# Where the first norm's sums of squares are made: ScalarE on token-major rows instead of GpSimd on transposed ones

## The chip, the cores and the metric

The kernel runs on one core of one Trainium2 chip. Its time is the device time of one execution in microseconds (us); of the kernel before, three runs are shown: 1096.92, 1096.26 and 1096.07 us, with a median of 1096.26 us.

In the rows of the trace the engines are PE (TensorE, matrix products), PEld (its weight loads), DVE (VectorE), ACT (ScalarE), POOL (GpSimd) and SP (SyncE, which issues nearly all DMAs; SPq is its queue). A line such as L109 is a line of the kernel's source.

## The reference, cut to what matters

One encoder layer on 256 tokens of width 2048, all in float32. Its first step is the one that the change touches:

```python
def rms_norm(x, g):
    y = xf * lax.rsqrt(jnp.mean(xf * xf, axis=-1, keepdims=True) + NORM_EPS)
    return (y * g).astype(x.dtype)

h = rms_norm(x, norm1_g)
proj = h @ w_in                     # 2048 x 4640: q, k, v, the gated part's q, k, v, gate, two low ranks
...                                 # windowed attention on one half, gated linear attention on the other
x = x + concat(o_attn, o_gla) @ w_out
x = x + conv_gated_ffn(rms_norm(x, norm2_g), w_up, conv_w, conv_b, w_down)
```

The norm needs, for each token, the sum of the squares of its 2048 values. Since that sum only scales a token's row, the kernel multiplies `x * norm1_g` with `w_in` first and applies 1/rms when the products leave PSUM.

## The kernel before, in words

Every product is made of operands split in two parts (a high part in a reduced format and the rest), three matmuls for one. A weight tile therefore goes through the same steps everywhere, in the helper `weights`: SP loads up to 512 KB into one of four `raw` buffers (L104), ACT writes the high part `hi` (L108, four buffers), DVE writes `lo = raw - hi` (L109, three buffers), and PE takes both. A `raw` buffer is free for the next load when ACT and DVE have read it. A tile's name tells its place: `rikv`, `hikv`, `likv` are raw, high and low of the input projection's first chunk of columns (k and v), `riqa`, `hiqa`, `liqa` those of its second and third chunk (queries).

The input projection runs over ten chunks of columns. Each chunk goes over 16 k-tiles of 128 rows. The first chunk has four units of one k-tile and six of two (called units 0 to 9 here); the second has eight units of two k-tiles (units q0 to q7 here). One k-tile takes six matmuls of 128x512. With the units of the first chunk SP also loads x, transposed (`xts`, L145); ACT scales and rounds it (`hh`, L148) and DVE makes the rest (`hl`, L149).

Hooks put other work between the units: `at(chunk, unit, fn)` calls `fn` before that unit's weights are asked for. There, `token_square(0)` and `(1)` make the squares of all transposed x on GpSimd (L173) and add them by halves (L174 to L176); `token_norm` sums over partitions by eight narrow matmuls with ones (`pn`, L183) and takes the root (`inv_sqrt`, L168 on DVE and L169 on GpSimd); `load_consts` loads the constants `cst_sb` and `prm_sb`; `store(0, ...)` brings the first chunk out of PSUM with the factor `rstd1` (L236). A scheduler orders the instructions on each engine from these calls; the splits of weights and the evacuations have a raised priority.

After the ten chunks come the attention pieces that are woven between them, the output projection (L584 to L586), the up projection with convolution (L632, L633) and the down projection (L667 to L669). PE takes instructions strictly in the order that the schedule gives, and so do the other engines and SP's queue.

Of the kernel before, what the change touches and what calls it, by code (L numbers as in the profile page):

```python
# [8 lines left out]
F32 = mybir.dt.float32  # L9
F32R = mybir.dt.float32r  # L10
BF16 = mybir.dt.bfloat16
U32 = mybir.dt.uint32
AF = mybir.ActivationFunctionType
ALU = mybir.AluOpType
AX = mybir.AxisListType
PSUM = bass.MemoryType.PSUM

A = slice(None)
P = 128
T = 256  # L20
DM = 2048
# [6 lines left out]
EPS = 1e-6  # L28
WCOLS = 1024

# Column chunks of the input projection: (name, [(first column, width), ...], whole width).
IN_CHUNKS = [
    ("kv", [(1024, 512)], 512),
    ("qa0", [(0, 512)], 512),
# [9 lines left out]


def in_units(ci):
    """k-tiles of each weight unit of a chunk of the input projection."""
    return [1] * 4 + [2] * 6 if ci == 0 else [3] * 5 + [1] if ci in (3, 4) else [2] * 8


# Small constants and parameters, by column.
C_COS, C_SIN, C_MASK, C_MF, C_MB = 0, 256, 512, 1024, 1280
C_QG, C_QGS, C_KG, C_KGS = 1536, 1664, 1792, 1920
NCST = 2048
# [5 lines left out]
def tile_hymba_layer(  # L60
# [15 lines left out]
    nc = tc.nc  # L76
    V, S, G, PE = nc.vector, nc.scalar, nc.gpsimd, nc.tensor
# [9 lines left out]
    def arena(shape, dt, name):  # L87
        return ar.tile(shape, dt, name=name, tag="ar")
# [7 lines left out]
    def aux(name):  # L96
        return paux.tile([P, 512], F32, name=name, tag="aux")
# [16 lines left out]
        V.tensor_tensor(lo, src, hi.bitcast(F32), ALU.subtract)  # L114

    def product(d, a, b, start=True, stop=True):
        """d (+)= a^T b, of operands in two parts each."""
        PE.matmul(d, a[0], b[0], start=start, stop=False)
        PE.matmul(d, a[0], b[1], start=False, stop=False)
        PE.matmul(d, a[1], b[0], start=False, stop=stop)  # L120
# [1 line left out]
    def both(tiles, *index):  # L122
        return [x[index] for x in tiles]

# [1 line left out]
    g1 = pers.tile([P, NKT], F32, name="g1")  # L126
    nc.scalar.dma_start(out=g1, in_=n1)
    prm_sb = pers.tile([P, NPRM], F32, name="prm_sb")
# [7 lines left out]
    xts, hh, hl = [], [], []  # L136
# [3 lines left out]
        hl.append(arena([P, 8, T], F32R, f"hl{i}"))  # L140

    def load_x(kt, n):
        """n k-tiles of x, scaled by the first norm's weight and split."""
        i, o = kt // 8, kt % 8
        nc.sync.dma_start(out=xts[i][:, o : o + n], in_=xt[:, kt : kt + n])  # L145
        for j in range(n):
            with tc.high_priority(offset=1500):
                S.activation(hh[i][:, o + j], xts[i][:, o + j], AF.Copy, scale=g1[:, kt + j : kt + j + 1])  # L148
                V.scalar_tensor_tensor(  # L149
                    out=hl[i][:, o + j], in0=xts[i][:, o + j], scalar=g1[:, kt + j : kt + j + 1],  # L150
                    in1=hh[i][:, o + j].bitcast(F32), op0=ALU.mult, op1=ALU.subtract,
                )
# [7 lines left out]
    warm = aux("warm")  # L160
    for i in range(9):
        PE.matmul(warm[:, :P], ones, ones, start=True, stop=True)
    ssq1 = {}
    rstd1 = pers.tile([P, 2], F32, name="rstd1")

    def inv_sqrt(dst, src, mul, add, n):
        t = sm.tile([P, 32], F32, name="isq", tag="isq")
        V.tensor_scalar(t[:, :n], src, mul, add, op0=ALU.mult, op1=ALU.add)  # L168
        G.tensor_tensor(dst, t[:, :n], mhalf[:, :n], op=ALU.pow)  # L169

    def token_square(i):
        sq = arena([P, 8, T], F32, f"sqx{i}")
        G.tensor_tensor(sq, xts[i], xts[i], op=ALU.mult)  # L173
        G.tensor_tensor(sq[:, 0:4], sq[:, 0:4], sq[:, 4:8], op=ALU.add)  # L174
        G.tensor_tensor(sq[:, 0:2], sq[:, 0:2], sq[:, 2:4], op=ALU.add)
        G.tensor_tensor(sq[:, 0], sq[:, 0], sq[:, 1], op=ALU.add)  # L176
        ssq1[i] = sq[:, 0]

    def token_norm():
        pn = aux("pn")  # L180
        for t in range(2):
            for i in range(2):
                PE.matmul(pn[:, 2 * t : 2 * t + 2], ssq1[i][:, t * P : t * P + P], ones[:, 0:2], start=(i == 0), stop=(i == 1))  # L183
        inv_sqrt(rstd1, pn[:, 0:4:2], 1.0 / DM, EPS, 2)

    cst_sb = arena([P, NCST], F32, "cst_sb")
    dec_sb = arena([P, 4, 384], F32R, "dec_sb")
# [11 lines left out]
    def load_wa():  # L199
        nc.sync.dma_start(out=wa_sb, in_=wa)  # L200

# [1 line left out]
    in_first = [0]  # L203

    hooks = {}
# [1 line left out]
    def at(ci, u, fn, *args):  # L207
        hooks.setdefault((ci, u), []).append((fn, args))
# [26 lines left out]
        with tc.high_priority(offset=1500):  # L235
            S.activation(dst, src, func, scale=rstd1[:, t : t + 1])  # L236

# [1 line left out]
    rope_kg = arena([P, 2, 1024], F32, "rope_kg")  # L239
    rope = rope_kg[:, 0].rearrange("p (a b c d) -> p a b c d", a=2, b=2, c=2)  # L240
    kg_sb = rope_kg[:, 1].rearrange("p (t c) -> p t c", t=2)
# [107 lines left out]
        if h % 2 == 1:  # L349
            split(oah[:, h - 1 : h + 1], oal[:, h - 1 : h + 1], po.rearrange("p (k s) -> p k s", k=2))  # L350

# [1 line left out]
    lr_sb = pers.tile([P, 2, 32], F32, name="lr_sb")  # L353
    gkT = arena([P, 2, GH, T], F32, "gkT")
    gh = arena([P, 2, 1024], F32R, "gh")
# [59 lines left out]
                gkT[:, 1, :, t * P : t * P + P], pq.rearrange("p (h s) -> p h s", h=GH), AF.Copy, scale=float(P) ** -0.5  # L415
            )

    # The blocks of e: for a key, -F3, the levels, B3; for a query, -B3, the levels, F3. By direction and tile of
    # tokens: (first column in the bank, role, first column in e, width, sign).
    PARTS = (  # L420
# [19 lines left out]
            V.tensor_tensor(e, e, gkT[:, role, h, t * P : t * P + P].unsqueeze(1).broadcast_to([P, 4, P]), ALU.mult)  # L440

    def mix(h):
        """The decayed products of head h: A^T [s, t] over all pairs of tokens."""
        es = arena([P, 2, 2, 4, P], F32, f"es{h}")
        scaled(h, 0, es)
        yield
        scaled(h, 1, es)
        yield

        def blk(role, t, what):  # L450
            return es[:, role, t, (0, 1 + t, 2 - t, 3)[what]]

        p1 = aux(f"p1{h}")
        p2 = aux(f"p2{h}")
        for s in range(2):
            for t in range(2):
                lv = 2 if s == t else 1
                PE.matmul(p1[:, (2 * s + t) * P : (2 * s + t + 1) * P], blk(0, s, lv), blk(1, t, lv), start=True, stop=True)
        for f in range(2):
            for t in range(2):  # L460
                PE.matmul(p2[:, (2 * f + t) * P : (2 * f + t + 1) * P], blk(0, t, 3 * f), blk(1, t, 3 - 3 * f), start=True, stop=True)
        at = work([P, 4, P], F32, f"at{h}", "sc", 3)
        S.activation(at.rearrange("p a s -> p (a s)"), p1, AF.Copy)
        diag = at[:, 0::3]
        for f, c in enumerate((C_MF, C_MB)):
            V.copy_predicated(
                diag, cst_sb[:, c : c + 256].bitcast(U32).rearrange("p (a s) -> p a s", a=2),
                p2[:, 2 * f * P : (2 * f + 2) * P].rearrange("p (a s) -> p a s", a=2),
            )
        split(atr[0][:, h], atr[1][:, h], at)  # L470
# [26 lines left out]
                PE.transpose(pt[:, e * T + t * P : e * T + t * P + P], o[:, t, e * P : e * P + P], ident)  # L497
        split(ogh[:, 2 * h : 2 * h + 2], ogl[:, 2 * h : 2 * h + 2], pt.rearrange("p (k s) -> p k s", k=2))

# [1 line left out]
    def store(ci, ps):  # L501
        """What a chunk of the projection goes to."""
        for t in range(2):
            if ci >= 8:
                c = ci - 8
                d = sg[:, t, c * 512 : c * 512 + 512]
                evac(d, ps[t], t, AF.Silu)
                dv = d.rearrange("p (h e) -> p h e", h=2)
                V.tensor_tensor(dv, dv, gn.unsqueeze(1).broadcast_to([P, 2, 256]), ALU.mult)
            elif ci == 3:  # L510
                evac(lr_sb[:, t], ps[t][:, 0:32], t)
                evac(kg_sb[:, t, 0:240], ps[t][:, 32:272], t)
            else:
                evac(
                    (kv_sb[:, t], qa_sb[:, 0, t], qa_sb[:, 1, t], None, kg_sb[:, t, 240:512],
                     gq_sb[:, t], vg[:, t, 0:512], vg[:, t, 512:1024])[ci], ps[t], t,
                )
            if ci in (6, 7):
                sl = slice((ci - 6) * 512, (ci - 5) * 512)
                split(vgr[0][:, t, sl], vgr[1][:, t, sl], vg[:, t, sl])  # L520
# [1 line left out]
    running = {}  # L522

    def go(*names):
        """Emit the next stage of each of the named pieces."""
        for name in names:
            if name not in running:
                fn = {"A": attend, "Q": queries, "M": mix, "R": retrieve}.get(name[0])
                running[name] = fn(int(name[1])) if fn else {"k": keys, "g": gates, "gk": gla_keys, "gq": gla_queries}[name]()
            next(running[name], None)  # L530
# [2 lines left out]
        at(0, u, load_x, u, 1)  # L533
    for u in range(4, 10):
        at(0, u, load_x, 2 * u - 4, 2)
    at(0, 7, token_square, 0)
    at(1, 1, token_square, 1)
    at(1, 2, token_norm)
    at(1, 2, load_consts)
    at(1, 4, rope_tables)  # L540
    at(1, 4, go, "k")
    at(2, 0, go, "k")
    at(2, 2, load_decay, 0)
    at(2, 4, load_decay, 1)
# [11 lines left out]
    for (ci, u), names in plan.items():  # L556
        at(ci, u, go, *names.split())
    first_ps = project(0)
    at(1, 3, store, 0, first_ps)
    for ci in range(1, len(IN_CHUNKS)):  # L560
        store(ci, project(ci))

# [1 line left out]
    x1 = [arena([P, 2, 2, 512], F32, f"x1{i}") for i in range(2)]  # L564
    xs = [arena([P, 4, 2, T], F32R, f"xs{i}") for i in range(4)]
    ssq2 = pers.tile([P, 2, 4], F32, name="ssq2")
    first = 0
# [47 lines left out]
    rbc = pers.tile([P, T], F32, name="rbc")  # L615
    V.tensor_copy(rbc, pb[:, :T])

# [1 line left out]
    gts = [arena([P, 2, 4, T], F32R, f"g{i}") for i in range(NFF // 4)]  # L619
    first = 0  # L620
    for f in range(NFF):
# [28 lines left out]
        S.activation(gt[:, 0, f % 4], cs[1], AF.Copy)  # L650
        V.tensor_tensor(gt[:, 1, f % 4], cs[1], gt[:, 0, f % 4].bitcast(F32), ALU.subtract)

# [1 line left out]
    first = 0  # L654
    for c in range(4):
        ps = [acc(f"pd{c}{t}") for t in range(2)]
# [61 lines left out]


def _units(w, sizes):  # L720
    """[K, n] -> units of a few k-tiles, each [128 partitions, k-tiles * n] in one run."""
    n, k, parts = w.shape[1], 0, []
    for per in sizes:
        parts.append(w[k : k + per * P].reshape(per, P, n).transpose(1, 0, 2).reshape(-1))
        k += per * P
    return np.concatenate(parts)
# [54 lines left out]
```

## Time and profile before

| what | value |
|---|---|
| median of three runs | 1096.26 us |
| span of the profiled execution, first to last instruction | 1094.4 us |
| PE busy | 1080.4 us (99%) |
| DVE busy | 783.6 us (72%) |
| ACT busy | 529.7 us (48%) |
| POOL busy | 31.2 us (3%) |
| mean DMA rate | 185 GB/s |

The profile gives the profiled execution's span and no further time of its own; the median of the runs stands 1.9 us above that span. A busy PE says only that a matmul was in flight. The share is a mean over the whole span: of the page's 40 slices of 27 us each, the first has PE at 7 tenths, the second at 8 and all later ones but the last at 9 (90% or more).

### The profile page before, as it was taken

Reading aid. Unit: us, or ns where it says so; the run is one execution under the profiler, and the core shown is the slowest. Engines: PE = TensorE matmul, PEld = TensorE weight load, DVE = VectorE, ACT = ScalarE, POOL = GpSimd, SP = SyncE. Lnnn points to the kernel's source line nnn. Section 1 sums busy time; section 2 is a strip of 40 time slices with the busy share of each in tenths; the row PEclk is TensorE's granted clock in tenths of the full one; section 3 lists DMA queues with packets and bytes.
Section 4 is the critical chain, followed back from the end, with each engine's and each line's share of the span. In section 5 each row is a group of like instructions: output and inputs, shape, how many; then the busy total and the mean of one; then the engine's idle time right before and its main releaser. Section 6 shows DMA issues by size and latency. Waiting matters only on the chain.

```text
span 1094.4 us, 14985 instructions
## 1 busy us (share of the span) xinstructions
PE 1080.4 (99%) x5616; PEld 921.1 (84%) x5616; DVE 783.6 (72%) x1173; ACT 529.7 (48%) x780; POOL 31.2 (3%) x24
## 2 busy tenths in 40 slices
PE   7899999999999999999999999999999999999998
PEld 6789888888888888888888888888888888888886
DVE  7788777756555888888888888888888544444443
ACT  6345566764445544444444444444444433333331
POOL 4311000010000000000000000000000000000000
PEclk9999999999999999999999999999999999999999
DMA  8565544436556655655565565555565656666662
GB/s 302 173 201 165 165 154 148 139 117 187 201 194 219 200 184 184 191 186 184 189 186 184 189 187 182 190 190 179 189 191 181 195 195 210 196 214 196 210 193 79
DMA packets 58040, 202.96 MB, mean 185 GB/s; under 512 B 6576, under 2 KB 7600, under 8 KB 57840
## 3 DMA queue, kind: packets, MB, share of 16 engines
q1 hardware_dynamic: 57680, 201.87, 58.2%
q8 instruction: 44, 0.72, 0.3%
q14 instruction: 28, 0.23, 0.1%
q10 hardware_dynamic: 288, 0.14, 0.0%
HBM read 199.89 MB, written 2.10 MB: 185 GB/s over the span
## 4 chain that ended last, share of the span: by engine, by line
PE 97%; DVE 1%; DMA 1%; ACT 0%; issue 0%; SPq 0%; DVEq 0%; ACTq 0%
PE pu L632 30%; PE pu L633 15%; PE pd L667 7%; PE pd L669 7%; PE pd L668 7%; PE po L586 3%; PE po L584 3%; PE po L585 3%; PE pvg L228 1%; PE pvg L229 1%; PE pqa L229 1%; PE pgt L230 1%; PE pgt L228 1%; PE pvg L230 1%; PE pqa L230 1%; PE pgt L229 1%
## 5 line engine op out<-in xcount | busy, mean ns | idle before, releaser
L632 PE MATMUL pu<-xs,hu 128*128 128x512 f32 x1408 | 497.4, 399 | 0.0
L633 PE MATMUL pu<-xs,lu 128*128 128x256 f32 x1408 | 395.3, 281 | 0.0
L632 PEld LDWEIGHTS pu<-xs,hu 128*128 128x128 f32 x1408 | 264.4, 188 | 65.7
L108 ACT ACTIVATE hu<-ru 128x1024 fp32r<-128x1024 f32 x176 | 186.9, 1062 | 253.0 <-PE pu L632 145.6
L633 PEld LDWEIGHTS pu<-xs,lu 128*128 128x128 f32 x1408 | 266.0, 189 | 0.2
L109 DVE TENSOR_TENSOR lu<-ru,hu 128x1024 fp32r<-128x1024 f32 x176 | 215.3, 1224 | 47.4 <-PE pu L633 41.2
L109 DVE TENSOR_TENSOR ld<-rd,hd 128x1024 fp32r<-128x1024 f32 x88 | 107.8, 1225 | 117.5 <-PE pd L668 112.2
L108 ACT ACTIVATE hd<-rd 128x1024 fp32r<-128x1024 f32 x88 | 93.6, 1064 | 143.8 <-PE pd L669 136.7
L668 PE MATMUL pd<-ld,g 128*128 128x512 f32 x352 | 136.9, 389 | 0.0
L667 PE MATMUL pd<-hd,g 128*128 128x512 f32 x352 | 136.9, 389 | 0.0
L669 PE MATMUL pd<-hd,g 128*128 128x512 f32 x352 | 136.9, 389 | 0.0
L669 PEld LDWEIGHTS pd<-hd,g 128*128 128x128 f32 x352 | 66.1, 188 | 13.8
L668 PEld LDWEIGHTS pd<-ld,g 128*128 128x128 f32 x352 | 66.1, 188 | 13.6
L667 PEld LDWEIGHTS pd<-hd,g 128*128 128x128 f32 x352 | 66.1, 188 | 13.6
L109 DVE TENSOR_TENSOR lo<-ro,ho 128x1024 fp32r<-128x1024 f32 x32 | 39.0, 1224 | 36.3 <-ACT ho L108 23.8
L108 ACT ACTIVATE ho<-ro 128x1024 fp32r<-128x1024 f32 x32 | 33.9, 1061 | 44.5 <-DMA ro<-in_wo_dram 30.7
L636 DVE TENSOR_TENSOR u<-u,pu 128x256 f32<-128x256 f32 x88 | 37.0, 421 | 13.8 <-ACT u L635 13.3
L643 DVE SCALAR_TENSOR_TENSOR c<-u,prm_sb,c 128x255 f32<-128x255 f32 x88 | 42.5, 484 | 3.0
L640 DVE SCALAR_TENSOR_TENSOR c<-u,prm_sb,c 128x255 f32<-128x255 f32 x88 | 42.0, 478 | 0.1
L639 DVE TENSOR_SCALAR c<-u,prm_sb 128x256 f32<-128x256 f32 x88 | 36.2, 412 | 3.0
L637 DVE TENSOR_TENSOR u<-u,rbc 128x256 f32<-128x256 f32 x88 | 37.1, 422 | 1.5
L635 ACT ACTIVATE u<-pu 128x256 f32<-128x256 f32 x88 | 32.1, 365 | 0.0
(225 smaller groups left out, 1425.7 us busy)
## 6 DMA issues: line engine op xcount, KB each, us to landing
ru<-in_wu_dram SPq DMA_DIRECT2D x176, 512.0 KB, 3.5
rd<-in_wd_dram SPq DMA_DIRECT2D x88, 512.0 KB, 3.9
ro<-in_wo_dram SPq DMA_DIRECT2D x32, 512.0 KB, 3.6
riqa<-in_wi_dram SPq DMA_DIRECT2D x16, 512.0 KB, 4.1
rivg<-in_wi_dram SPq DMA_DIRECT2D x16, 512.0 KB, 3.5
rigt<-in_wi_dram SPq DMA_DIRECT2D x16, 512.0 KB, 3.5
riqg<-in_wi_dram SPq DMA_DIRECT2D x8, 512.0 KB, 4.0
rilk<-in_wi_dram SPq DMA_DIRECT2D x10, 408.0 KB, 3.6
```

What stands on the lines that cost most here:

```text
L108: S.activation(hi[:, :cols], r[:, :cols], AF.Copy)
L109: V.tensor_tensor(lo[:, :cols], r[:, :cols], hi[:, :cols].bitcast(F32), ALU.subtract)
L632: PE.matmul(pu, wh, x2, start=(u == 0 and k == 0), stop=False)
L633: PE.matmul(pu[:, T:], wl, x2[:, :T], start=False, stop=(u == 1 and k == 7))
L636: V.tensor_tensor(ut, ut, pu[:, :T], ALU.add)
L637: V.tensor_tensor(ut, ut, rbc, ALU.mult)
L639: V.tensor_scalar(c, ut, cw[:, 1, n : n + 1], cb[:, n : n + 1], op0=ALU.mult, op1=ALU.add)
L640: V.scalar_tensor_tensor(out=c[:, 1:T], in0=ut[:, 0 : T - 1], scalar=cw[:, 0, n : n + 1], in1=c[:, 1:T], op0=ALU.mult, op1=ALU.add)
L643: V.scalar_tensor_tensor(out=c[:, 0 : T - 1], in0=ut[:, 1:T], scalar=cw[:, 2, n : n + 1], in1=c[:, 0 : T - 1], op0=ALU.mult, op1=ALU.add)
L667: PE.matmul(ps[t], a, wh, start=(kt == 0), stop=False)
L668: PE.matmul(ps[t], a, wl, start=False, stop=False)
L669: PE.matmul(ps[t], b, wh, start=False, stop=(kt == NFF - 1))
```

## The change

The squares are no longer made from the transposed x on GpSimd. Four further loads bring x token-major (`xr`, 512 KB each, 128 tokens by two halves of 512 columns) into the `raw` buffers, before the first four units of the second chunk. ACT squares each half and adds along the row (`accum_out`), 128x512 in one instruction, eight of them. DVE reduces the four partial sums of a token; the sum over partitions on PE falls away. The hooks behind it move two units later: the norm and the constants from unit 2 of the second chunk to unit 4, the rope tables and the keys from 4 to 6, the store of the first chunk from 3 to 5. The diff's other edits are comments.

```diff
-    ssq1 = {}
+    ssq1 = pers.tile([P, 2, 4], F32, name="ssq1")
...
-    def token_square(i):
-        sq = arena([P, 8, T], F32, f"sqx{i}")
-        G.tensor_tensor(sq, xts[i], xts[i], op=ALU.mult)
-        G.tensor_tensor(sq[:, 0:4], sq[:, 0:4], sq[:, 4:8], op=ALU.add)
-        G.tensor_tensor(sq[:, 0:2], sq[:, 0:2], sq[:, 2:4], op=ALU.add)
-        G.tensor_tensor(sq[:, 0], sq[:, 0], sq[:, 1], op=ALU.add)
-        ssq1[i] = sq[:, 0]
+    def token_square(c):
+        r = raw(f"xq{c}")
+        nc.sync.dma_start(out=r, in_=xr[c])
+        for t in range(2):
+            junk = work([P, 512], BF16, "junkx", "jk", 1)
+            S.activation(junk, r[:, t * 512 : t * 512 + 512], AF.Square, accum_out=ssq1[:, t, c : c + 1])
...
     def token_norm():
-        pn = aux("pn")
-        for t in range(2):
-            for i in range(2):
-                PE.matmul(pn[:, 2 * t : 2 * t + 2], ssq1[i][:, t * P : t * P + P], ones[:, 0:2], start=(i == 0), stop=(i == 1))
-        inv_sqrt(rstd1, pn[:, 0:4:2], 1.0 / DM, EPS, 2)
+        s1 = sm.tile([P, 2], F32, name="s1", tag="s1")
+        V.tensor_reduce(s1, ssq1, AX.X, ALU.add)
+        inv_sqrt(rstd1, s1, 1.0 / DM, EPS, 2)
...
-    at(0, 7, token_square, 0)
-    at(1, 1, token_square, 1)
-    at(1, 2, token_norm)
-    at(1, 2, load_consts)
-    at(1, 4, rope_tables)
-    at(1, 4, go, "k")
+    for c in range(4):
+        at(1, c, token_square, c)
+    at(1, 4, token_norm)
+    at(1, 4, load_consts)
+    at(1, 6, rope_tables)
+    at(1, 6, go, "k")
...
-    at(1, 3, store, 0, first_ps)
+    at(1, 5, store, 0, first_ps)
```

On SP's queue, from the parameters that follow the last load of transposed x on, the kernel before has these loads. `rikv8` and `rikv9` are the raw weights of units 8 and 9, `riqa00` to `riqa04` those of q0 to q4, `cst_sb` the constants (1024 KB):

```order
L192 DMA prm_sb_78<-in_prm_dram 128x760
L104 DMA rikv8_291<-in_wi_dram 128x1024
L104 DMA rikv9_314<-in_wi_dram 128x1024
L104 DMA riqa00_334<-in_wi_dram 128x1024
L191 DMA cst_sb_102<-in_cst_dram 128x2048
L104 DMA riqa01_357<-in_wi_dram 128x1024
L104 DMA riqa02_385<-in_wi_dram 128x1024
L104 DMA riqa03_405<-in_wi_dram 128x1024
L104 DMA riqa04_463<-in_wi_dram 128x1024
```

The changed kernel has at the same place, with `xq0` to `xq3` for the rows of x:

```order
L190 DMA prm_sb_78<-in_prm_dram 128x760
L104 DMA rikv8_287<-in_wi_dram 128x1024
L189 DMA cst_sb_103<-in_cst_dram 128x2048
L104 DMA rikv9_310<-in_wi_dram 128x1024
L174 DMA xq0_330<-in_xr_dram 128x1024
L104 DMA riqa00_336<-in_wi_dram 128x1024
L174 DMA xq1_354<-in_xr_dram 128x1024
L104 DMA riqa01_360<-in_wi_dram 128x1024
L174 DMA xq2_378<-in_xr_dram 128x1024
L104 DMA riqa02_384<-in_wi_dram 128x1024
L174 DMA xq3_402<-in_xr_dram 128x1024
L104 DMA riqa03_408<-in_wi_dram 128x1024
```

The constants have moved ahead of unit 9's weights, and each of q0 to q3 has a load of x ahead of its own.

On ACT, at the end of the first chunk, the kernel before has the high parts of units 8 and 9 and of the second chunk one after the other:

```order
L108 ACTIVATE hikv8_293<-rikv8_291 128x1024
L108 ACTIVATE hikv9_316<-rikv9_314 128x1024
L108 ACTIVATE hiqa00_336<-riqa00_334 128x1024
L108 ACTIVATE hiqa01_359<-riqa01_357 128x1024
L108 ACTIVATE hiqa02_387<-riqa02_385 128x1024
```

The changed kernel has there:

```order
L108 ACTIVATE hikv8_289<-rikv8_287 128x1024
L108 ACTIVATE hikv9_312<-rikv9_310 128x1024
L177 ACTIVATE junkx_332,ssq1_101<-xq0_330 128x512
L177 ACTIVATE junkx_334,ssq1_101<-xq0_330 128x512
L108 ACTIVATE hiqa00_338<-riqa00_336 128x1024
L177 ACTIVATE junkx_356,ssq1_101<-xq1_354 128x512
L177 ACTIVATE junkx_358,ssq1_101<-xq1_354 128x512
L108 ACTIVATE hiqa01_362<-riqa01_360 128x1024
```

Two squares stand ahead of each of the high parts of q0 to q3. On PE the eight matmuls `pn` are gone from the third unit of the second chunk; apart from them and from swaps of neighbours up to the first attention scores, PE's order is that of before, and it is the same from there to the end.

## Rows read from the trace of the kernel before

**Rows 1.** The waits of PE: us in total, times, longest us.
```profile
PE pkv L229 <- DVE likv L109: 8.2, 3, 3.5
...
PE pkv L228 <- ACT hikv L108: 0.6, 1, 0.6
```

**Rows 2.** Timeline, PE: start us, us, engine, line, operation [idle before <-releaser].
```profile
16.47 0.80 PE L229 MATMUL pkv<-likv,hh 128*128 128x512 f32 x1 [3.54 <-DVE likv L109]
...
19.89 0.40 PE L229 MATMUL pkv<-likv,hh 128*128 128x512 f32 x1
...
29.89 0.80 PE L229 MATMUL pkv<-likv,hh 128*128 128x512 f32 x1 [3.49 <-DVE likv L109]
...
35.61 0.50 PE L229 MATMUL pkv<-likv,hh 128*128 128x512 f32 x1 [1.12 <-DVE likv L109]
35.95 0.40 PE L230 MATMUL pkv<-hikv,hl 128*128 128x512 f32 x1
...
40.75 0.62 PE L228 MATMUL pqa<-hiqa,hh 128*128 128x512 f32 x2
...
43.47 0.62 PE L228 MATMUL pqa<-hiqa,hh 128*128 128x512 f32 x2
...
46.19 0.62 PE L228 MATMUL pqa<-hiqa,hh 128*128 128x512 f32 x2
46.65 0.95 PE L183 MATMUL pn<-ones,sqx 128*128 128x2 f32 x8
47.46 0.49 PE L229 MATMUL pqa<-liqa,hh 128*128 128x512 f32 x1
```

**Rows 3.** Timeline, DVE, same columns.
```profile
12.17 4.25 DVE L109 TENSOR_TENSOR likv<-rikv,hikv 128x1024 fp32r<-128x1024 f32 x1 [1.00 <-ACT hikv L108]
...
17.13 1.21 DVE L109 TENSOR_TENSOR likv<-rikv,hikv 128x1024 fp32r<-128x1024 f32 x1
...
20.19 6.36 DVE L149 SCALAR_TENSOR_TENSOR hl<-xts,g,hh 128x256 fp32r<-128x256 f32 x2
26.48 3.36 DVE L109 TENSOR_TENSOR likv<-rikv,hikv 128x1024 fp32r<-128x1024 f32 x1
```

**Rows 4.** Timeline, POOL, same columns.
```profile
11.73 3.60 POOL L173 TENSOR_TENSOR sqx<-xts 128x2048 f32<-128x2048 f32 x1 [11.29 <-DMA xts<-in_xt_dram]
18.78 4.96 POOL L173 TENSOR_TENSOR sqx<-xts 128x2048 f32<-128x2048 f32 x1 [3.44 <-DMA xts<-in_xt_dram]
23.69 5.06 POOL L174 TENSOR_TENSOR sqx<-sqx 128x1024 f32<-128x1024 f32 x2
```

**Rows 5.** Stretches: busy us (instructions) by engine, PEclk, DMA share, GB/s.
```profile
9.00:12.00 3.00, 3.00 (x15) 2.37 (x13) 2.17 (x5) 2.49 (x5) 0.27 (x1) 1.00 1.03 388
12.00:15.00 3.00, 0.92 (x4) 0.30 (x2) 2.83 (x1) 2.78 (x6) 3.00 (x1) 1.00 0.99 361
15.00:18.00 3.00, 1.53 (x4) 1.26 (x5) 3.00 (x4) 2.44 (x4) 0.34 (x1) 0.71 1.04 411
18.00:21.00 3.00, 3.00 (x11) 2.41 (x10) 3.00 (x5) 2.08 (x6) 2.22 (x1) 0.72 1.03 374
24.00:27.00 3.00, 2.40 (x11) 1.67 (x9) 3.00 (x3) 1.35 (x2) 3.00 (x2) 1.00 0.69 288
...
30.00:33.00 3.00, 3.00 (x7) 2.38 (x8) 3.00 (x3) 0.00 (x0) 3.00 (x3) 0.50 0.55 180
```

**Rows 6.** Timeline, ACT, same columns as Rows 2.
```profile
20.99 1.06 ACT L108 ACTIVATE hikv<-rikv 128x1024 fp32r<-128x1024 f32 x1 [0.92 <-DMA rikv<-in_wi_dram]
```

**Rows 7.** DMA landings of second-chunk weights; squares and reduction of the second norm.
```profile
DMA to landing us min/median/max: 3.3/4.2/5.1
...
L591 ACT ACTIVATE junk<-x x8: 611/613/631, 285.0 to 354.2; 128x512 bf16<-128x512 f32 x8
L591 ACT ACTIVATION_READ_ACCUMULATOR junk<-x x8: 186/186/189, 285.5 to 354.7; 128x1 f32 x8
...
L608 DVE TENSOR_REDUCE s<-ssq x1: 161/161/161, 354.9 to 354.9; 128x2 f32<-128x8 f32 x1
```

## The prediction, written before the changed kernel ran

> **What bounds the kernel now.** I read the page's slices first: PE is at 90% or more from the third slice to the last but one, so its order of matmuls is the time, and only the first 50 us hold anything to win. Then the list of PE's waits: but for the start it holds four, three of them for the low part of first-chunk weights from DVE, 8.2 us together [rows 1]. Then the timelines of PE, DVE and POOL over 10 to 50 us. PE waits 3.54 us before 16.47, 3.49 before 29.89 and 1.12 before 35.61, and never again [rows 2]. DVE is not idle there: the low part that takes 1.21 us at 17.13 took 4.25 at 12.17 and 3.36 at 26.48, and two `hl` at 20.19 took 6.36 together [rows 3]. Each of these lies over a long POOL instruction: POOL's first square runs from 11.73 for 3.60, so to 15.33, and 15.33 + 1.09 is where DVE's 4.25 us end, 16.42; the second square and the first halving run from 18.78 on without a gap [rows 4]. DVE waits inside its instruction for GpSimd. Last, the table by stretches: PE's granted clock is 0.50, the 1.2 GHz level, in 30 to 33 us after the wait of 3.49, and 0.71 and 0.72 as means over 15 to 21 after that of 3.54 [rows 5]; after the 1.12 us wait the next start follows 0.34 later and the matmul takes 0.40 [rows 2], so the clock was not lowered there.
>
> **The change part by part. What it gives.** At the 2.4 GHz level, 12 matmuls (a unit of two k-tiles) take 43.47 - 40.75 = 2.72 us, 0.227 each [rows 2].
>
> First wait: without POOL the low part of unit 4 ends at 12.17 + 1.21 = 13.38 instead of 16.42, and PE goes on 0.05 later, at 13.43 instead of 16.47: 3.04 us.
>
> The rest of the chunk: from 16.47 to 40.75 PE did 10 matmuls of unit 4 and five units, 70 matmuls, in 24.28 us. At 0.227 they are 15.87: 8.41 us. In it are the two later waits and about 1.6 us of half clock behind each long one (16.47 to 19.89 holds 8 starts, 3.42 us for 1.82).
>
> The matmuls `pn`: the next matmul would start at 46.19 + 2 x 0.227 = 46.64 and starts at 47.46 [rows 2]: 0.82 us.
>
> Together 12.27 us, the most that there is. POOL's own 19 us (3.60 + 4.96 + 5.06 here and the two smaller halvings behind) lie on no path other than DVE's.
>
> **What it costs.** The eight squares have their like in the second norm, 0.61 and 0.19 us for the accumulator [rows 7], 0.80 each and 1.6 us for one load. The reduction is 0.16 us on DVE. Both lie beside matmuls; ACT was busy 1.35 of 3 us in 24 to 27 [rows 5]. What counts is when q0 to q3 get their weights, since each follows a 512 KB load of x on SP's queue and two squares on ACT.
>
> The DMA engines are at a share of 0.99 or more from 9 to 21 us, at 388, 361, 411 and 374 GB/s, 384 in the mean [rows 5]. An earlier issue there brings nothing earlier: unit 8's weights land at 20.95 as before (ACT starts on them at 20.99 after a DMA wait [rows 6]). Behind them at 384 GB/s: the constants 2.73 us, then 1.37 us for each load of 512 KB. Unit 9's weights land at 25.05; ACT 1.06, DVE 1.21 and two hand-overs of 0.03 give the low part at 27.35. PE ends unit 8 at 13.43 + 10 x 0.227 + 4 x 2.72 = 26.58, wants the low part two matmuls later, at 27.03, and waits to 27.40: 0.37 us. It ends unit 9 at 29.67.
>
> q0: x lands at 26.42, q0's weights at 27.79; ACT squares to 28.02 and rounds to 29.08, the low part is there at 30.32, wanted at 30.12: 0.25 us with the hand-over.
>
> q1 to q3: four raw buffers hold two pairs. A weight buffer is free when DVE has read it; the next load in it lands 3.3 to 4.2 us after its issue [rows 7], then 1.06 and 1.24: 5.6 to 6.5 us for every two units, against 5.44 on PE. That is 0.1 to 0.5 us a unit. No row shows this mix of loads: the least is nothing, if the ring runs ahead; I take 0.15, near the shorter landing, since the loads are spaced as PE takes them. Three units: 0.45.
>
> q4: the factor `rstd1` is now late enough that ACT brings the first chunk out (two 128x512, some 1.3 us) between the high parts of q3 and q4, and DVE has the rope tables ahead of q4's low part. Before, the same work lay under a pipeline that was already ahead. I take 0.4, from nothing to 1.3. Behind q4 two loads no longer compete and the pipeline gets ahead again.
>
> Costs: 0.37 + 0.25 + 0.45 + 0.4 = 1.5. None of these waits is near the 3.5 us after which rows show a lowered clock, and all are at or under the 1.12 us after which they don't.
>
> **Sum.** 12.27 - 1.5 = 10.8 us. After that PE's order is the old one and PE waited for nothing, so the shift goes through to the end. The profiled span of 1094.4 becomes 1083.6; the 1.9 us between the span and the median of the runs stay: 1096.26 - 10.8 = 1085.5 us. With no cost at all it is 1084.0. With 361 GB/s (0.63 us before unit 9, 0.35 before q0), 0.5 a unit and 1.3 at q4 the costs are 3.8 and the time 1087.8.
>
> The stretches of 388, 361, 411 and 374 GB/s have a page against them. The Trainium skill, "DMA: Bandwidth & Descriptors", section "Where 436 GB/s comes from", has transfers from HBM bound at about 358 GB/s for a core. By that a pair of loads would take 2.93 us, 0.21 more than PE's unit, and the constants with unit 9's weights 4.39: 0.66 before unit 9, four times 0.21 and 0.4, together 1.9 instead of 1.5, so 1085.9. Three of the four stretches lie clearly above it, so I keep 384.
>
> **The rivals.** *Loads come in gaps (16 in 100).* The rate holds only while enough is queued; where POOL held buffers back it was 288 [rows 5]. From 20.95 to the landing of q3's weights pass 5.77 MB (constants, unit 9, four pairs), 20.0 us at 288, so 41.0, and the low part is there at 43.3. PE wants it at 26.58 + 4 x 2.72 + 0.45 = 37.9: 5.4 late, with q4 5.8. Net 6.5: 1089.8. For it: buffers are shared by twice the loads. Against: two pairs are always allowed in flight.
>
> *DVE is not freed (3 in 100).* If its long instructions have another cause, only `pn` goes: 0.82, 1095.4. Against it: the ends fit to 0.1 us, and between POOL's rows the same instruction takes 1.21.
>
> *The pairs go in lockstep (6 in 100), slower than before.* SP issues in order, and a load of x that waits for a square stands ahead of weights. If only one pair is under way, a pair takes 4.2 to land and 1.6 of squares before ACT reaches the weights: 5.8 us against 2.72, 3.1 lost on each of four units, and each such wait is nearly as long as those after which PE ran at 1.2 GHz for 1.6 us more: 18.8 lost, with unit 9 and q4 19.6. Net -7.3: 1103.6. It decides from 5.6 us a pair, a wait of 2.9 on each, and sooner if the clock falls behind waits as short as these. Against: four buffers, so half of 5.8 a pair, 2.9.
>
> That the squares stay on GpSimd is excluded: its rows are gone from the order.
>
> **How the numbers follow.** The forecast, 1084.0 to 1087.8, has 75 in 100. To leave out no more than 2 in 10 I go from 1083.8 up to 1089.8, the middle of the gap case. A difference under 0.2%, 2.2 us, is about what a measurement can't tell from none: the third case lies there. Faster 0.91 (75 + 16), same 0.03, slower 0.06.
>
> **What would show it.** Right: every low part of 128x1024 on DVE at about 1.2 us from 12 us on; PE's first matmul on the queries at about 29.7 instead of 40.75; PE's clock at 1.00 in every stretch; waits under 0.5 us at unit 9 and at q0 to q4. The gap case shows a DMA share under 0.9 from 24 to 36 us and PE waiting for `hiqa`; the lockstep shows it at q1 to q3 with 3 us each and the clock at 0.5 behind; the case of an unfreed DVE shows its 4 us rows without POOL. Wrong altogether it would be if PE, which now reaches the key transposes and the attention earlier, began to wait there for DVE's chain.

## The result, and the profile after

The changed kernel takes 1085.78 us (median of four runs, 1085.29 to 1088.95); the kernel before took 1096.59 us on the same chip in the same rounds. The ratio is 0.9903 with a 95% interval of 0.9891 to 0.9915: 10.8 us faster, where 10.8 were forecast.

The profiled execution is the one that took 1088.95 us, with a span of 1087.2. The other three have spans of 1083.5 to 1084.1. One thing in its profile, the late load described below, is therefore likely its own.

First the page's line of busy times, after:

```profile
PE 1077.7 (99%) x5608; PEld 918.2 (84%) x5608; DVE 769.5 (71%) x1174; ACT 535.0 (49%) x796; POOL 11.3 (1%) x16
```

POOL went from 31.2 to 11.3 us, DVE from 783.6 to 769.5: DVE has one more reduction to do and is busy 14 us less, since its busy time held waits. Next, the waits of PE (us in total, times, longest), against [rows 1]:

```profile
PE pqa L226 <- ACT hiqa L108: 1.5, 1, 1.5
...
PE pkv L226 <- ACT hikv L108: 1.0, 2, 0.5
PE po L583 <- DVE lo L109: 0.8, 1, 0.8
PE pqa L227 <- DVE liqa L109: 0.5, 1, 0.5
PE pkv L227 <- DVE likv L109: 0.5, 1, 0.5
```

The 8.2 us for `likv` have become 0.5. The wait for `hikv` went from 0.6 to 1.0. New are 1.5 and 0.5 at the queries and, much later, 0.8 in the output projection. The timeline of DVE, against [rows 3], shows why the first went:

```profile
12.10 1.23 DVE L109 TENSOR_TENSOR likv<-rikv,hikv 128x1024 fp32r<-128x1024 f32 x1 [1.00 <-ACT hikv L108]
...
19.03 1.67 DVE L149 SCALAR_TENSOR_TENSOR hl<-xts,g,hh 128x256 fp32r<-128x256 f32 x4
24.96 1.23 DVE L109 TENSOR_TENSOR likv<-rikv,hikv 128x1024 fp32r<-128x1024 f32 x1 [2.44 <-ACT hikv L108]
...
38.13 0.16 DVE L181 TENSOR_REDUCE s<-ssq 128x2 f32<-128x8 f32 x1 [0.37 <-ACT junkx L177]
```

The instruction that took 4.25 us at 12.17 takes 1.23 at 12.10; four `hl` take 1.67 where two took 6.36. The reduction that replaces `pn` takes 0.16. POOL, against [rows 4], does nothing from the memsets at the start to the root of the norm:

```profile
38.57 0.70 POOL L169 TENSOR_TENSOR rstd<-isq,mhalf 128x2 f32<-128x2 f32 x1 [38.13 <-DVE isq L168]
```

The timeline of PE, against [rows 2]:

```profile
13.38 0.50 PE L227 MATMUL pkv<-likv,hh 128*128 128x512 f32 x1 [0.53 <-DVE likv L109]
...
29.42 0.62 PE L226 MATMUL pqa<-hiqa,hh 128*128 128x512 f32 x2
...
36.55 0.73 PE L226 MATMUL pqa<-hiqa,hh 128*128 128x512 f32 x2 [1.53 <-ACT hiqa L108]
37.81 0.50 PE L227 MATMUL pqa<-liqa,hh 128*128 128x512 f32 x1 [0.53 <-DVE liqa L109]
...
38.85 0.63 PE L228 MATMUL pqa<-hiqa,hl 128*128 128x512 f32 x1
...
41.80 0.62 PE L226 MATMUL pqa<-hiqa,hh 128*128 128x512 f32 x2
```

The first product with a low part in unit 4 starts at 13.38 instead of 16.47, and the queries at 29.42 instead of 40.75: 11.33 us ahead. With `pn` gone (0.82) that would be 12.15. Then q2, due at 34.86 (12 matmuls in 2.72 behind 32.14), starts at 36.55, waits once more, and runs at half clock, 0.42 from start to start, until q3 starts at 41.80 instead of 37.58: 4.22 us given back in one unit. What is left, 7.93, agrees with the 8.0 by which the output projection starts earlier (253.2 for 261.2). The wait of 0.8 there leaves 7.2, the difference of the two spans (1094.4 - 1087.2).

The stretches (us, busy time and instructions of PE, PEld, DVE, ACT, POOL, granted clock, DMA share, GB/s), against [rows 5]:

```profile
12.00:15.00 3.00, 2.35 (x9) 1.64 (x10) 2.90 (x4) 2.93 (x7) 0.00 (x0) 1.00 1.04 417
...
18.00:21.00 3.00, 3.00 (x15) 2.49 (x14) 2.69 (x5) 2.17 (x5) 0.00 (x0) 1.00 1.05 436
...
33.00:36.00 3.00, 2.02 (x9) 1.33 (x8) 0.00 (x0) 0.81 (x3) 0.00 (x0) 1.00 0.87 288
36.00:39.00 3.00, 1.92 (x6) 1.26 (x7) 1.75 (x4) 2.85 (x6) 0.43 (x1) 0.89 0.69 268
39.00:42.00 3.00, 3.00 (x9) 2.34 (x8) 2.93 (x10) 2.74 (x5) 0.27 (x1) 0.54 0.97 350
```

Up to 21 us the loads ran at 417 and 436 GB/s, faster than before. At 33 to 36 DVE did nothing at all and ACT 0.81 us: both were waiting for q2's weights. The chain that ended last shows them, start and duration in us, with ACT's split right behind:

```profile
29.63 5.72 DMA riqa<-in_wi_dram
35.45 1.06 ACT hiqa L108
```

They took 5.7 us from issue to landing, where the median of the query weights in this execution is 3.6.

### The profile page after: what moved, and what is told of

It is laid out like the page before. It is cut to its first block, busy times and chain, and to the rows that moved or that the text cites. A ratio compares the mean times of both kernels' runs of the same rounds, so it can differ in the third digit from the quotient of the medians.

```text
span 1087.2 us, 14981 instructions
## 1 busy us (share of the span) xinstructions
PE 1077.7 (99%) x5608; PEld 918.2 (84%) x5608; DVE 769.5 (71%) x1174; ACT 535.0 (49%) x796; POOL 11.3 (1%) x16
## 4 chain that ended last, share of the span: by engine, by line
PE 96%; DMA 2%; DVE 1%; ACT 0%; issue 0%; DVEq 0%; SPq 0%; ACTq 0%
PE pu L630 30%; PE pu L631 15%; PE pd L667 7%; PE pd L665 7%; PE pd L666 7%; PE po L583 3%; PE po L584 3%; PE po L582 3%; PE pvg L226 1%; PE pvg L227 1%; PE pgt L228 1%; PE pgt L226 1%; PE pvg L228 1%; PE pgt L227 1%; PE pqa L227 1%; PE pqa L228 1%
## 5 line engine op out<-in xcount | busy, mean ns | idle before, releaser
L109 DVE TENSOR_TENSOR lo<-ro,ho 128x1024 fp32r<-128x1024 f32 x32 | 38.8, 1223 | 38.4 <-ACT ho L108 27.8
```

The source lines that it names most:

```text
L109: V.tensor_tensor(lo[:, :cols], r[:, :cols], hi[:, :cols].bitcast(F32), ALU.subtract)
```

## The experiments

Two theories. **A**: GpSimd's squares, reading the on-chip memory SBUF, held DVE's two-input instructions, and that hold was PE's whole loss; the loads and squares that replaced them cost little because they lie beside matmuls that take longer. **B**: the gain comes from the order that the edit brought (hooks two units later, other neighbours), and DVE's long rows had another cause. The runs under "what it costs" ask how much the four loads of x cost, and whether q2's late weights are the rule.

**The changed kernel again, twice** (no edit; the second time beside the runs of loads and constants).

> The changed kernel itself, once more, for a second profile. My theory (GpSimd's squares held DVE up; the x loads cost a little back): 1085.3 to 1086.0 us in most executions, and a profiled span near 1083.7 in which the waits of PE from 20 us on come to under 1.5 us in all; the first profile's 1.53 and 0.53 us waits at the third unit of the second chunk, with the lowered clock behind, are one late landing and not the rule. Rival (the wait at that unit belongs to the change): every profile shows it, with 1.5 us or more there.

> The changed kernel as the measure for the three kernels that run beside it. 1085.3 to 1086.3 us, with single executions some 3 us higher where a load of the second chunk lands late.

Measured: 1085.93 us (ratio 0.9901, 0.9886 to 0.9915) and 1085.19 (0.989, 0.9877 to 0.9904), spans 1083.8 and 1083.6. The timeline of PE, the first time, the rows behind 20 us with a wait:

```profile
27.82 0.50 PE L227 MATMUL pkv<-likv,hh 128*128 128x512 f32 x1 [0.23 <-DVE likv L109]
...
33.72 0.50 PE L227 MATMUL pqa<-liqa,hh 128*128 128x512 f32 x1 [0.15 <-DVE liqa L109]
```

and the second time, with the starts of q0 and q6 and one low part of q2:

```profile
29.00 0.61 PE L226 MATMUL pqa<-hiqa,hh 128*128 128x512 f32 x2
...
32.96 0.50 PE L227 MATMUL pqa<-liqa,hh 128*128 128x512 f32 x1 [0.31 <-DVE liqa L109]
...
35.94 0.50 PE L227 MATMUL pqa<-liqa,hh 128*128 128x512 f32 x1
36.28 0.40 PE L228 MATMUL pqa<-hiqa,hl 128*128 128x512 f32 x1
...
39.39 0.50 PE L227 MATMUL pqa<-liqa,hh 128*128 128x512 f32 x1 [0.39 <-DVE liqa L109]
...
47.44 0.62 PE L226 MATMUL pqa<-hiqa,hh 128*128 128x512 f32 x2
```

No late q2, no half clock. The waits shown add up to 0.38 and 0.70, but the starts of the units tell more. From q0 to q6 there are six units, 16.32 us at 2.72; in the second repeat they take 18.44, so 2.12 are lost. The rest lies around matmuls that got their low part just in time: behind such a matmul the next start follows 0.34 later, where back to back it is 0.227, and ahead of some of them, as at 35.94, PE's list has no wait. The wait is then PEld's, which loads the weights:

```profile
35.94 0.19 PEld L227 LDWEIGHTS pqa<-liqa,hh 128*128 128x128 f32 x1 [0.35 <-DVE liqa L109]
```

In the first repeat the loss is 0.53 in unit 9 and 1.13 from q0 to q6. Three of the twelve executions of the changed kernel were profiled, and one of these shows the late load; no other of the twelve took more than 1086.71 us.

**GpSimd's work put back, its result unused.** The changed kernel, with the squares and halvings of before on GpSimd at the old hooks.

```diff
+    def pool_square(i):
+        sq = arena([P, 8, T], F32, f"sqx{i}")
+        G.tensor_tensor(sq, xts[i], xts[i], op=ALU.mult)
+        G.tensor_tensor(sq[:, 0:4], sq[:, 0:4], sq[:, 4:8], op=ALU.add)
...
+    at(0, 7, pool_square, 0)
...
+    at(1, 1, pool_square, 1)
```

> The changed kernel with GpSimd's squares and adds put back at their old places as idle extra work, their result unused. My theory: the whole price of them returns, 3.04 + 8.41 us of the prediction's terms, from a floor of 1084.0, with the x loads hidden under it or not: 1095.3 to 1097.5 us, and DVE's low parts of 4 and 3 us are there again over POOL's rows. Rival (the gain came from the missing narrow matmuls, the moved hooks or the new order, not from DVE): 1085.3 to 1086.5 us.

Measured: 1096.64 us, ratio 1.0001 (0.9992 to 1.0011). The whole gain is gone. Timeline of DVE, then of PE:

```profile
12.13 4.24 DVE L109 TENSOR_TENSOR likv<-rikv,hikv 128x1024 fp32r<-128x1024 f32 x1 [1.54 <-ACT hikv L108]
...
18.22 6.36 DVE L149 SCALAR_TENSOR_TENSOR hl<-xts,g,hh 128x256 fp32r<-128x256 f32 x2
24.50 3.37 DVE L109 TENSOR_TENSOR likv<-rikv,hikv 128x1024 fp32r<-128x1024 f32 x1
```

```profile
16.42 0.79 PE L234 MATMUL pkv<-likv,hh 128*128 128x512 f32 x1 [3.54 <-DVE likv L109]
27.92 0.50 PE L234 MATMUL pkv<-likv,hh 128*128 128x512 f32 x1 [3.08 <-DVE likv L109]
```

The rows of before are back (4.25, 6.36, 3.36 in [rows 3]), with the hooks, the squares on ACT and the orders of PE, ACT and DVE those of the changed kernel. B falls.

**The squares left out.** The kernel before without squares and without loads of x rows; the norm's sums come from ones, so its output is not the layer's.

```diff
     def token_square(i):
-        sq = arena([P, 8, T], F32, f"sqx{i}")
...
-        ssq1[i] = sq[:, 0]
+        pass
...
-                PE.matmul(pn[:, 2 * t : 2 * t + 2], ssq1[i][:, t * P : t * P + P], ones[:, 0:2], start=(i == 0), stop=(i == 1))
+                PE.matmul(pn[:, 2 * t : 2 * t + 2], ones, ones[:, 0:2], start=(i == 0), stop=(i == 1))
```

> The kernel before without its squares: the sums of squares are left out and the narrow matmuls take ones instead, no rows of x are loaded, hooks stay where they were. My theory: nothing but DVE's freedom and the matmuls that now stand at the start: 1096.3 less 12.27, plus about 0.4 before unit 9, 1084.0 to 1085.0 us. Rival (order and hooks make the gain): 1095 us or more.

Measured: 1085.0 us, ratio 0.9893 (0.9877 to 0.991). Waits of PE:

```profile
PE pkv L224 <- DVE likv L109: 1.0, 2, 0.5
```

With nothing in the place of GpSimd's squares the kernel gains as much as the change does: the interval holds all three ratios of the changed kernel. It isn't the pure floor, though: without squares to wait for, the scheduler moved `pn` to the start and the constants ahead of unit 9's weights, and one of the two waits of 0.5 is at unit 9.

**Does GpSimd's writing hold DVE, or its reading?** The changed kernel with ten fills of 128x2048 on GpSimd, and with four one-input multiplications of 128x2048, each beside the first chunk.

```diff
+        for _ in range(5):
+            G.memset(sq, 1.0)
```

```diff
+        G.tensor_scalar(sq, xts[i], 2.0, None, op0=ALU.mult)
+        G.tensor_scalar(sq, xts[i], 3.0, None, op0=ALU.mult)
```

> The changed kernel with ten GpSimd fills of 128x2048 where the squares stood (they write tiles that nobody reads, and read nothing). If DVE waits for GpSimd's reads of memory (both of DVE's splits read two tiles): 1085.3 to 1086.2 us and low parts of 1.2 us beside POOL's rows. If any long GpSimd instruction holds DVE: as many long low parts as fills that meet one, 1088 us or more.

> The changed kernel with four GpSimd multiplications of a 128x2048 tile by a constant where the squares stood: they read one tile and write one that nobody reads. The fills, which read nothing, left DVE at 1.2 us a low part. If a GpSimd instruction that reads memory holds DVE's two-input splits, with one input as with two: low parts and hl of 2 us and more over POOL's rows, 1087 to 1092 us. If only two-input GpSimd instructions do: 1085.2 to 1086.3 us.

Measured: 1086.19 us, ratio 0.9907 (0.9893 to 0.9922), with the fills; 1096.56 (ten runs, 1091.67 to 1097.82), ratio 0.9987 (0.9975 to 0.9999), with the multiplications. Timelines of POOL and of DVE under the fills:

```profile
0.73 17.53 POOL L182 MEMSET sqx<- 128x2048 f32 x10 [0.29 <-POOLq L774]
```

```profile
14.83 1.23 DVE L109 TENSOR_TENSOR likv<-rikv,hikv 128x1024 fp32r<-128x1024 f32 x1 [0.51 <-ACT hikv L108]
```

and under the multiplications:

```profile
12.45 5.37 POOL L181 TENSOR_SCALAR sqx<-xts 128x2048 f32<-128x2048 f32 x1 [12.02 <-DMA xts<-in_xt_dram]
18.95 5.38 POOL L181 TENSOR_SCALAR sqx<-xts 128x2048 f32<-128x2048 f32 x1 [1.13 <-DMA xts<-in_xt_dram]
```

```profile
12.80 4.37 DVE L109 TENSOR_TENSOR likv<-rikv,hikv 128x1024 fp32r<-128x1024 f32 x1 [1.93 <-ACT hikv L108]
...
19.02 4.25 DVE L149 SCALAR_TENSOR_TENSOR hl<-xts,g,hh 128x256 fp32r<-128x256 f32 x2
23.19 1.21 DVE L109 TENSOR_TENSOR likv<-rikv,hikv 128x1024 fp32r<-128x1024 f32 x1
24.33 4.29 DVE L149 SCALAR_TENSOR_TENSOR hl<-xts,g,hh 128x256 fp32r<-128x256 f32 x2
```

POOL was busy from 0.73 to 18.26 with fills and DVE took its 1.23; under a POOL instruction that reads one tile the same instruction took 4.37. So A gets narrower: a GpSimd instruction that reads holds DVE, with one input as with two; one that only writes does not. The size of the second was missed: I expected 1087 to 1092, since I took one-input work to be shorter than the squares. At 5.37 us a row it is longer than the square's 3.60 [rows 4], but the rows are not the measure: the low part at 23.19 took 1.21 us although POOL's row of 18.95 runs to 24.33, so the hold ended before the row did (the profile's page calls POOL's rows rough). What counts is how much longer than its free time DVE was busy. With the multiplications that is 3.2 (low part, 1.21 free), 3.4 and 3.4 (two `hl`, 0.87 free) and 3.4 us (four `hl` at 29.67, 5.07 for 1.67), 13.4 in all; before it is 3.0, 5.5, 2.2 and 3.0, 13.7 in all. The holds are alike, and so are the times, 1096.56 and 1096.59.

### What the new work costs

**No loads of x.** The changed kernel, with the squares reading the resident transposed x, so that the sums are not the norm's.

```diff
-        r = raw(f"xq{c}")
-        nc.sync.dma_start(out=r, in_=xr[c])
+        r = xts[c // 2].rearrange("p k s -> p (k s)")
...
-            S.activation(junk, r[:, t * 512 : t * 512 + 512], AF.Square, accum_out=ssq1[:, t, c : c + 1])
+            n = (2 * (c % 2) + t) * 512
+            S.activation(junk, r[:, n : n + 512], AF.Square, accum_out=ssq1[:, t, c : c + 1])
```

> The changed kernel whose eight squares take their input from the transposed x that lies in memory (so the sums are not the norm's, and no rows of x are loaded); all else as it is. My theory (the x loads cost 0.25 before q0 and 0.45 at q1 to q3, the squares on ACT nothing): 0.3 to 1.0 us under the changed kernel beside it, no wait of PE at q0 to q3. Rival (the loads are hidden, the late norm or ACT makes the rest): within 0.2 us of it.

Measured: 1085.74 us, ratio 0.9897 (0.9883 to 0.991), 0.55 above the changed kernel beside it. A miss, and inconclusive on the price: with no load to wait for, the scheduler moved the squares into the first chunk, from 10.62 us on, one of them at 14.40 ahead of a high part that PE was about to need. The timeline of PE shows a wait there that the changed kernel hasn't:

```profile
17.37 0.50 PE L227 MATMUL pkv<-likv,hh 128*128 128x512 f32 x1 [0.53 <-DVE likv L109]
```

No wait is left at q0 to q3.

**Each x block loaded twice**, eight loads instead of four (with a 128x1 copy on ACT for each, so that the first of a pair is read).

```diff
-        r = raw(f"xq{c}")
-        nc.sync.dma_start(out=r, in_=xr[c])
+        for _ in range(2):
+            r = raw(f"xq{c}")
+            nc.sync.dma_start(out=r, in_=xr[c])
+            touch = sm.tile([P, 1], F32, name=f"touch{c}", tag="act0")
+            S.activation(touch, r[:, 0:1], AF.Copy)
```

> The changed kernel with each row block of x loaded twice into the shared buffers, the first copy read by one tiny ACT instruction. If the DMA engines set the pace of q0 to q3, as I think, a unit needs three loads, 4.1 us against PE's 2.72: 1.4 us more a unit, 4 to 6 us in all, up to 8 with a lowered clock behind a long wait: 1089.5 to 1094 us. Rival (loads have room there): under 1087 us.

Measured: 1092.63 us, ratio 0.996 (0.9946 to 0.9974), 7.44 more than the changed kernel beside it, 1.86 for each further load with its copy. Waits of PE, and a stretch (columns as above):

```profile
PE pqa L229 <- ACT hiqa L108: 2.9, 3, 1.1
PE pqa L230 <- DVE liqa L109: 2.1, 4, 0.5
```

```profile
36.00:39.00 3.00, 2.47 (x11) 1.80 (x10) 0.63 (x1) 1.54 (x5) 0.00 (x0) 1.00 0.91 270
```

With the four loads that the change adds, the two repeats lost 1.13 and 2.12 us from q0 to q6, 0.3 to 0.5 for each load if all of it is put down to them (the last experiments show that it is not the loads alone); four more lose 1.86 each. Little room is left beside PE's matmuls.

**Buffers of their own for x.** The rows of x go to two tiles outside the `raw` ring, so their loads wait for no weight buffer.

```diff
+    xq = [None]
...
-        r = raw(f"xq{c}")
+        if c % 2 == 0:
+            xq[0] = arena([P, 2, 1024], F32, f"xq{c}")
+        r = xq[0][:, c % 2]
```

> The changed kernel with the rows of x in two large tiles of their own instead of the shared raw buffers. Nothing holds these loads now, so in the schedule all four and the constants go out ahead of q0's weights, and two of them ahead of unit 9's. My theory (what counts is how many bytes stand ahead of the weights on the queue): unit 9's weights land two loads later less the constants, so about as now, but q0's 3.1 MB behind unit 8, at about 30 to 32 us, PE waits 2 to 5 us at q0 and perhaps at a lowered clock behind: 1087 to 1091 us. Rival (four shared buffers are the limit, own ones free it): 1085.2 us or less.

Measured: 1089.33 us, ratio 0.9924 (0.991 to 0.9937): slower than the changed kernel. The loads of x and the constants now all went out ahead of q0's weights. Timeline of PE:

```profile
33.00 0.73 PE L230 MATMUL pqa<-hiqa,hh 128*128 128x512 f32 x2 [2.72 <-ACT hiqa L108]
34.26 0.80 PE L231 MATMUL pqa<-liqa,hh 128*128 128x512 f32 x1 [0.52 <-DVE liqa L109]
34.86 0.63 PE L232 MATMUL pqa<-hiqa,hl 128*128 128x512 f32 x1
```

What counted here is how many bytes stand ahead of a unit's weights on SP's queue, not how many buffers there are: the shared ring of four had kept the loads of x from running ahead.

**Loads spread, constants held back, both.** Three kernels with the squares on ACT as in the changed one. The first loads x ahead of q0, q2, q4 and q5, with the norm, the store, the rope tables and the keys later:

```diff
-    for c in range(4):
-        at(1, c, token_square, c)
-    at(1, 4, token_norm)
-    at(1, 4, load_consts)
...
+    for c, u in enumerate((0, 2, 4, 5)):
+        at(1, u, token_square, c)
+    at(1, 6, token_norm)
+    at(1, 6, load_consts)
...
-    at(1, 5, store, 0, first_ps)
+    at(1, 6, store, 0, first_ps)
```

The second makes the constants wait, by a tiny copy that reads the partial sums, until all four loads of x are squared:

```diff
     def load_consts():
+        V.tensor_copy(cst_sb[:, 0:4], ssq1[:, 0, 0:4])
         nc.sync.dma_start(out=cst_sb, in_=cst)
```

The third has the spread loads, and constants that are called for at unit 3 and wait for the first partial sum alone.

> The changed kernel with the x loads before units 0, 2, 4 and 5 of the second chunk instead of 0 to 3, constants where they are. If the better time of the version with both edits (1083.74 against 1085.19 us) comes from the spacing: 1083.5 to 1084.3 us. If from the constants: 1085.0 to 1085.8 us.

> The changed kernel with the constants held back behind the four first partial sums, x loads where they are. If the better time of the version with both edits comes from the constants, which no longer stand ahead of unit 9's weights: 1083.6 to 1084.4 us. If from the spacing: 1085.0 to 1085.8 us; and if the rope tables now come too late for the keys, PE waits at their transposes and it is over 1086.

> A version that might beat the changed kernel: the x loads before units 0, 2, 4 and 5 of the second chunk instead of 0 to 3, and the constants held back until the first square is made, so that unit 9's weights go ahead of them. By my terms the waits before unit 9 (0.23 in the undisturbed profile), q0 and q1 to q3 go and the load that lands late has more slack: 0.3 to 1.0 us under the changed kernel beside it and fewer slow executions. Rival: the later norm makes the keys late, PE waits at their transposes, and it is even or slower.

Measured: 1084.18 us (ratio 0.9883, 0.9869 to 0.9896), 1083.75 (0.9878, 0.9865 to 0.9892) and 1083.74 (0.9879, 0.9865 to 0.9892). The third ran beside the changed kernel, 1.45 us faster than it, and no run of the one reaches the other's (up to 1084.66, from 1084.69). The first two did not run beside it: their ratios overlap its own (0.9877 to 0.9904), but their slowest execution, 1084.59, lies under the fastest of its twelve, 1084.69. The waits of PE in the second:

```profile
PE warm L162 <- DVE mhalf L157: 1.1, 1, 1.1
PE pkv L227 <- ACT hikv L108: 0.8, 1, 0.8
PE pkv L228 <- DVE likv L109: 0.5, 1, 0.5
```

Behind 13.4 us no wait is left; from q0 (29.35) to q6 (46.05) it loses 0.38. In this kernel the constants go out behind q5's weights instead of ahead of unit 9's, and the four loads of x are where the change put them: most of the 1.13 to 2.12 us lost from q0 to q6 therefore hangs on the constants and the loads together, not on the loads alone. Either edit brings the time to the 1084.0 at which the prediction had no cost left, and all three kernels were faster than the two that were given, by about 0.1% against the changed one.

## Why the prediction was right

**What the change gives: right, by the mechanism named.** The low part of unit 4 fell to 1.23 us where 1.21 was said; PE went on at 13.38 where 13.43 was said, 3.09 us for the term of 3.04. The rest of the first chunk took 16.04 us (13.38 to 29.42) where 15.87 and 0.37 were said. `pn` is gone. That DVE was held by GpSimd is shown by the work put back (ratio 1.0001) and by the squares left out (0.9893). That it takes a GpSimd instruction which reads is shown by the fills and the multiplications; one that reads without writing was not run. Where the prediction has the ends of POOL's rows as the ends of the hold, this fits the first square and not the multiplications. The Trainium skill, "SBUF — State Buffer", section "Who interferes with whom", says that a DVE instruction with two SBUF inputs contends with a GpSimd instruction that reads SBUF, not with one that only writes it; 4.37 us beside multiplications and 1.23 beside fills agree.

**What it costs: near as a sum in one profile of three, its places wrong.** I had 0.37 for unit 9 and 1.1 for q0 to q4, 1.5 in all. Read by unit starts, the two repeats give 0.53 and 1.13 (to q6), together 1.66; nothing and 2.12; and the profile after nothing and 4.22. Unit 9's weights were said to land at 25.05. ACT took them up at 23.87 and 23.95 where nothing was lost, and at 25.45 in the first repeat, where 0.53 was. The rate of 384 GB/s was low up to there: in the profile after, four stretches from 12 to 24 us ran at 410 to 436 GB/s. The 358 GB/s of the Trainium skill, "DMA: Bandwidth & Descriptors", section "Where 436 GB/s comes from", lies further off still. q0, at 0.25, lost 0.31 in the second repeat and nothing in the others. q1 to q3, at 0.45 together, lost 0.65, 0.26 and 0.71 there, 1.62; q4, at 0.4, lost 0.18. Most of it is not idle time that PE's list of waits shows, but matmuls whose weights came just in time. My term for q1 to q3 was too small, at least in part because I took the shorter landing, 3.3 us: in the second repeat the weights of q1 and q2 landed 4.2 and 3.9 us after their issue, and the three units lost 0.54 each, a little over the upper end of my 0.1 to 0.5. The term for q4 was too large. And I charged the constants to unit 9 and q0 alone: held back, they leave 0.38 us from q0 to q6, so they weigh on the units behind as well.

**The sum: 1085.5 said, 1085.78, 1085.93 and 1085.19 measured.** The three gains and the loss close on the trace to 0.4 us: for the second repeat 40.75 - 29.00 = 11.75, and 0.82, less 2.12, is 10.45; its output projection starts 10.6 earlier and its span is 10.8 shorter. That the difference came out at 10.8 to the digit is in part luck. In the second repeat the gain before any loss is 12.57 where 12.27 was said, since PE went on in unit 4 at 13.00 and not at 13.43, and the loss is 2.12 where 1.5 was said: two errors of opposite sign. The kernel before, too, has a median of 1096.59 over four runs where the prediction started from 1096.26.

**One statement failed: that PE's clock would be 1.00 in every stretch, since only waits near 3.5 us lower it.** In the profile after, waits of 1.53 and 0.53 us with two matmuls between them were followed by the 1.2 GHz level; so were 2.72 and 0.52 with buffers apart. Waits of 1.11 and 0.53, the same two matmuls between, were not, in the run with eight loads. The bound was too high for single waits as well: in the run with multiplications one of 2.33 us, with no second wait behind it, was followed by half clock (0.43 from start to start from 30.87 on, a granted clock of 0.63 over 30 to 33 us).

```profile
29.81 0.50 PE L232 MATMUL pkv<-likv,hh 128*128 128x512 f32 x1 [2.33 <-DVE likv L109]
...
30.87 0.63 PE L231 MATMUL pkv<-hikv,hh 128*128 128x512 f32 x1
```

One of 1.52 us there, at 35.94, was not (1.00 over 36 to 39 us). A late weight tile makes two waits in a row, one for the high part and one for the low; that 1.53 was followed by half clock with 0.53 behind it, and 1.52 alone was not, suggests that the second wait counts, but these are two cases in different surroundings. The price was small only because the case is rare: 4.2 us in one execution of twelve, some 0.35 in the mean.

**The rivals.** The gap case named two signs. A DMA share under 0.9 from 24 to 36 us came in all three profiles (0.85 after, 0.83 and 0.89 in the repeats, at 294, 306 and 319 GB/s), so the 384 did not hold behind 24 us, yet in the repeats PE had no wait for `hiqa` and the price was not paid. PE waiting for `hiqa` came in the one execution, with 4.2 us lost for the 5.8 it had. What delayed that load isn't settled: in the two other profiles its neighbours on the queue are the same, and in the second repeat it went out at 29.59, within 0.04 us of the late one, and took 3.9. The lockstep did not come; loading x twice shows how near it is, with 1.86 us for each further load.

## What to carry to other kernels

An engine that is on no path and 3% busy can still hold the engine that is: where the same instruction takes 1.2 us in one place and 4 in another, look at what reads SBUF beside it before looking at the instruction. When work is moved onto loads, count the bytes that stand ahead of the next weights on the queue and spread them; more buffers only let the wrong loads go first. And measure a loss by the starts of equal units: in one profile here two thirds of it stood in no wait of PE, but around weights that came just in time, where only the waits of PEld show it.

## What the runs showed of the hardware

- A one-input GpSimd multiplication of 128x2048 took 5.37 us, longer than a two-input square of the same tile with itself, 3.60 and 4.96 [rows 4]; a fill of that size took 1.75 (17.53 for ten). Each of the four multiplications cost DVE 3.2 to 3.4 us, and DVE was free again before POOL's row ended.
- Behind a matmul whose weight tile comes just in time the next start is 0.34 away instead of 0.227, about 0.11 us, also where PE's list has no wait; PEld's has it (2.6 us in five waits in the second repeat).
- Two waits of 1.53 and 0.53 us, two matmuls apart, were followed by the 1.2 GHz level for about 3.3 us (38.4 to 41.8), and so was a single one of 2.33; 1.11 and 0.53, and a single 1.52, were not.
- The loads of the one core ran at 436 GB/s over 18 to 21 us in the profile after, and at 430 and 439 in the repeats.
